# 1/rms spread one k step earlier, u_s copied out of PSUM by ScalarE, the first weight split moved ahead

## The chip, the cores and the metric

The kernel runs on one core of a Trainium2 chip. The metric is the device time of one execution in microseconds (us). Five engines work side by side, each through its own instructions in program order: PE (TensorE matmul, with PEld for its weight loads), DVE (VectorE), ACT (ScalarE), POOL (GpSimd) and SP (SyncE), whose queue issues every DMA of this kernel. An instruction that waits holds up everything behind it on its engine.

## The reference, cut to what matters

```python
h = rms_norm(x, pre_g)                       # x: 1024 x 1024, f32
proj = h @ w_in                              # cb | ca -> conv branch, u_s -> S5 branch, z and g gates
cu = ca * sigmoid(cb); cu = causal_depthwise_conv(cu)          # 31 taps
conv_out = (silu(layer_norm(cu)) * silu(z_c)) @ w_conv_out
y = gelu(s5(u_s)); y = y * sigmoid(y @ w_glu + b_glu)          # complex-diagonal state scan
ssm_out = (y * silu(z_s)) @ w_ssm_out
merged = sigmoid(g_c) * conv_out + sigmoid(g_s) * ssm_out
out = x + rms_norm(merged @ w_out, post_g)
```

## The kernel before, in words

Every f32 product is made of three passes of rounded operands: high part times high part, high times low, low times high. So each operand is split: ACT copies the high part (`xh`, `wh_...`), and DVE subtracts it from the original to get the low part (`xl`, `wl_...`). A product of one 128-channel block is 48 matmuls of 128x512: for each of 8 k steps a pair with (wh, xh), a pair with (wh, xl), a pair with (wl, xh).

The order is written out by hand in Python. A small clock object (`clk`) follows TensorE's time while the list `seq` of products is walked, and background chains (the S5 branch, the convolution taps, the LayerNorm) are put between the products' instructions when the clock says that their DVE cost and their delay have passed. A chain yields (cost, delay) pairs for that. Changing a delay therefore moves instructions in the program, not at run time.

The start has to overlap the norm with the first product. The three first u_s blocks (`usp0` to `usp2`, in PSUM) are multiplied from unnormalised x (raw x times the gain), 8 k steps of 9 passes. Meanwhile ACT squares x (`x_square`, on the second copy `xin`), DVE and POOL make 1/rms (`x_rms`, tile `r8t`), and in the eighth k step TensorE spreads it over the partitions (`x_spread`: matmuls into `rb`, then ACT copies `rb` to the tile `rbc`). Then

- `x_scale(k)` (DVE, L170) multiplies raw x by gain and `rbc`; `x_norm(k)` splits it anew (ACT `xh` L175, DVE `xl` L176), once the fourth u_s block `usp3` has used the raw `xh`, `xl` of that k;
- `us_out(m)` (DVE, L183) multiplies `usp{m}` by `rbc` out of PSUM into `usT{m}`, writes it to DRAM (`us_scratch`) and reads it back in 8 small DMAs as `U{m}` for S5;
- `wsplit_h`, `wsplit_l` (ACT L696, DVE L704) split the next weights of `order`: us3, cb0, ca0, gc0, cb1, ... ; `wload`, called at the end of `wsplit_l`, issues the load (`wr_...`) of the one two further on. There are two buffers for raw weights.

Products then follow as cb0, ca0, gc0, cb1, ca1, gc1, ... In `ln_stat(c)` the finished convolution block `acc{c}` is transposed by TensorE (`lnp{c}`) and DVE takes its statistics (`BN_STATS`). In `ln_chain` 1/std and mean are spread by TensorE (`lnr`, `lnm`), and DVE and ACT apply them to the eight blocks.

Of the kernel before, what the change touches and what calls it, by code (L numbers as in the profile page):

```python
# [10 lines left out]
AF = mybir.ActivationFunctionType  # L11
ALU = mybir.AluOpType
# [23 lines left out]
def tile_hybrid_block(  # L36
# [25 lines left out]
    V, A, G, PE = nc.vector, nc.scalar, nc.gpsimd, nc.tensor  # L62
# [14 lines left out]
    def T(name, dt=F32):  # L77
        return tp.tile([128, 1024], dt, tag="T", name=name)

    def PS(name, tag):  # L80
        return ps.tile([128, 1024], F32, tag=tag, name=name)

    def f32(t):
        return t.bitcast(F32)
# [27 lines left out]
    def load_xt(k):  # L112
        xraw[k] = T(f"xt{k}")
        nc.sync.dma_start(out=xraw[k], in_=xt[k])
# [4 lines left out]
    def us_weights(k2, parts=1):  # L119
        wusr[k2] = wp.tile([128, 1024], F32, tag="wraw", name=f"wusr{k2}", bufs=WRAW)  # L120
        n = 768 // parts
        for i in range(parts):
            nc.sync.dma_start(out=wusr[k2][:, i * n:(i + 1) * n], in_=w_us[k2][:, i * n:(i + 1) * n])
# [25 lines left out]
    def load_x(t):  # L149
        xin[t] = T(f"xin{t}")  # L150
        nc.sync.dma_start(out=xin[t], in_=xv[t])

    def x_square(t):
        xi = xin.pop(t)
        A.activation(out=xi, in_=xi, func=AF.Square, accum_out=ssq8[:, t:t + 1])
# [5 lines left out]
    def x_spread(rb):  # L161
        for t in range(8):
            PE.matmul(rb[:, t * 128:(t + 1) * 128], lhsT=r8t[:, t:t + 1].to_broadcast([128, 128]), rhs=ident,
                      start=True, stop=True)
        rbc = T("rbc")
        A.activation(out=rbc, in_=rb, func=AF.Copy)
        return rbc
# [10 lines left out]

    usU = {}

    def us_out(m, p, rbc):
        u = T(f"usT{m}")
        V.tensor_tensor(out=u, in0=p, in1=rbc, op=ALU.mult)  # L183
        clk.fg(1.2)
        nc.sync.dma_start(out=us_scr[m], in_=u)
        usU[m] = T(f"U{m}")
        src = us_scr[m].rearrange("(g h) (t n) -> t h g n", g=8, t=8)
        for t in range(8):
            nc.sync.dma_start(out=usU[m][16 * (7 - t):16 * (8 - t)].rearrange("p (g n) -> p g n", g=8), in_=src[t])
# [374 lines left out]
    stat_left, ln_done = [8], [False]  # L564

    def ln_stat(c):
        p = PS(f"lnp{c}", "aux")
        for t in range(8):
            PE.transpose(p[:, t * 128:(t + 1) * 128], acc[c][:, t * 128:(t + 1) * 128], ident)
        clk.now += 0.9  # L570
        yield 0.0, 2.0
        for t in range(8):
            V.bn_stats(out=st8[:, t, c, :], in_=p[:, t * 128:(t + 1) * 128])
            if t % 4 == 3:
                yield 0.9, 0.0
        stat_left[0] -= 1
        yield 0.0, 0.0
# [102 lines left out]
    def wload():  # L680
        if rnext[0] < len(order):
            u = order[rnext[0]]
            rnext[0] += 1
            src, kt = wsrc(*u)
            raw = wp.tile([128, 1024], F32, tag="wraw", name=f"wr_{u[0]}{u[1]}", bufs=WRAW)
            nc.sync.dma_start(out=raw[:, 0:kt * 128], in_=src)
            raws[u] = (raw, kt)

    def wsplit_h():
        if wnext[0] < len(order):  # L690
            u = order[wnext[0]]
            wnext[0] += 1
            raw, kt = raws.pop(u)
            n = kt * 128
            h = wp.tile([128, 1024], F32R, tag="wh", name=f"wh_{u[0]}{u[1]}", bufs=WHL)
            A.activation(out=h[:, 0:n], in_=raw[:, 0:n], func=AF.Copy)  # L696
            half[0] = (u, raw, h, n)

    def wsplit_l():
        if half[0]:  # L700
            u, raw, h, n = half[0]
            half[0] = None
            l = wp.tile([128, 1024], F32R, tag="wl", name=f"wl_{u[0]}{u[1]}", bufs=WHL)
            V.tensor_tensor(out=l[:, 0:n], in0=raw[:, 0:n], in1=f32(h[:, 0:n]), op=ALU.subtract)  # L704
            clk.fg(1.14 * n / 1024)
            wt[u] = (h, l)
            wload()
# [66 lines left out]
    def s5_chain():  # L774
        yield from s5_params(P5)
        for c in range(4):
            while not P5_ready[0]:
                yield 0.0, 0.5
            yield from s5_quarter(c, P5)
        for c in range(4):  # L780
            yh[c], yl[c] = T(f"yh{c}", F32R), T(f"yl{c}", F32R)
            A.activation(out=yh[c], in_=y32[c], func=AF.Copy)
            V.tensor_tensor(out=yl[c], in0=y32[c], in1=f32(yh[c]), op=ALU.subtract)
            yield 1.15, 0
        s5_done[0] = True
        yield 0.0, 0.0
# [5 lines left out]
    usp = {m: PS(f"usp{m}", "aux" if m == 2 else "mm") for m in range(3)}  # L792
# [3 lines left out]
    rbc = None  # L796
    for k in range(8):
        if k == 0:
            us_weights(2)
            load_xt(6)  # L800
            load_xt(7)
            for t in range(3):
                load_x(t)
            clk.add('s5', s5_chain())
        if k == 1:
            us_weights(3)
            for t in range(3, 8):
                load_x(t)
        if k == 2:
            for d_, s_ in ((chn, chan), (cw, conv_w), (iota, iota_in), (bgl, bglu), (bmt, bmat), (cmt, cmat),  # L810
                           (dmt, dmat)):
                nc.sync.dma_start(out=d_, in_=s_)
        if k + 2 < 8:
            x_raw(k + 2)
            if k % 2 == 0:
                us_split(k // 2 + 1, 0, 1)
        for t in {3: (0, 1), 4: (2, 3, 4), 5: (5, 6, 7)}.get(k, ()):
            x_square(t)
        if k == 5:
            x_rms()  # L820
        if k == 6:
            V.tensor_scalar(out=nb1, in0=chn[:, 0, :], scalar1=-1.0, scalar2=None, op0=ALU.mult)
            V.tensor_scalar(out=b2, in0=chn[:, 0, :], scalar1=2.0, scalar2=None, op0=ALU.mult)
            cwv = cw.rearrange("p c (r e) -> p c r e", e=2)
            V.tensor_tensor(out=hs, in0=cwv[:, :, :, 0], in1=cwv[:, :, :, 1], op=ALU.add)
            clk.fg(0.6)
        if k == 5:
            for _ in range(WRAW):
                wload()
        h, l = wus[k // 2]  # L830
        c0 = (k % 2) * 384
        kk = [slice(c0 + m * 128, c0 + m * 128 + 128) for m in range(3)]
        passes = ((h, xh), (l, xh), (h, xl))
        for n_, (m, i) in enumerate([(m, i) for i in range(3) for m in range(3)]):
            lhs, rhs = passes[i]
            for j in range(2):
                js_ = slice(j * 512, (j + 1) * 512)
                PE.matmul(usp[m][:, js_], lhsT=lhs[:, kk[m]], rhs=rhs[:, k, js_], start=(k == 0 and i == 0),  # L838
                          stop=(k == 7 and i == 2))
            if k == 7 and n_ == 0:  # L840
                rbc = x_spread(PS("rb", "aux"))
                wsplit_h()
                wsplit_l()
                clk.dve = max(clk.dve, clk.now + 1.5)
                for k_ in range(4):
                    x_scale(k_, rbc)
            clk.tick(0.45)
    us_out(0, usp[0], rbc)
    h, l = wt.pop(("us", 3))
    usp[3] = PS("usp3", "aux")  # L850
    for k in range(8):
        ks = slice(k * 128, (k + 1) * 128)
        for lhs, rhs, st, sp_ in ((h, xh, k == 0, False), (h, xl, False, False), (l, xh, False, k == 7)):
            for j in range(2):
                PE.matmul(usp[3][:, js(j)], lhsT=lhs[:, ks], rhs=rhs[:, k, js(j)], start=st, stop=sp_)
        x_norm(k)
        if k < 4:
            x_scale(k + 4, rbc)
        if k == 1:
            us_out(1, usp[1], rbc)  # L860
        if k == 3:
            wsplit_h()
            wsplit_l()
        clk.tick(1.296)
    us_out(2, usp[2], rbc)
    us_out(3, usp[3], rbc)
    P5_ready[0] = True
    clk.add('conv', conv_chain())

# [16 lines left out]
    for u in seq:  # L886
        kind, m = u
        report(u)
        if kind == "cb":
            p = proj(u)  # L890
# [5 lines left out]
        elif kind == "ca":  # L896
            p = proj(u)
# [6 lines left out]
        elif kind in ("gc", "zc"):  # L904
            p = proj(u)
# [8 lines left out]
        elif kind == "glu":  # L914
            p = product(f"pgl{m}", u, lambda k, j: yh[k][:, js(j)], lambda k, j: yl[k][:, js(j)])
# [5 lines left out]
        elif kind == "zs":  # L921
            p = proj(u)
# [11 lines left out]
        elif kind == "gs":  # L934
            p = proj(u)
# [4 lines left out]
        elif kind == "so":  # L940
            p = product(f"pso{m}", u, lambda k, j: y2h[k][:, js(j)], lambda k, j: y2l[k][:, js(j)])
# [26 lines left out]
        elif kind == "co":  # L968
# [5 lines left out]
            p = product(f"pco{m}", u, lambda k, j: cuh[:, k, js(j)], lambda k, j: cul[:, k, js(j)])  # L974
# [70 lines left out]
    for t in range(4, 7):  # L1045
        p = PS(f"po{t}", "aux" if t < 6 else "mm")
# [85 lines left out]
```

## Time and profile before

| | |
|---|---|
| median of 3 runs | 849.43 us (847.44 to 849.70) |
| the profiled execution | 848.62 us, of it 846.5 us span |
| PE busy | 820.1 us, 97% |
| DVE busy | 622.6 us, 74% |
| ACT busy | 276.1 us, 33% |
| DMA queue of SP | 90.17 MB |

The span is what the profile covers; the 2.1 us beside it lie before and after. PE busy is a modelled figure. A row of a timeline gives start, duration, engine, line, operation, out<-in, form and count, and in brackets the idle time of the engine just before it and what ended it. A row of the chain gives start, duration and what stood on the chain of waits that ended last.

### The profile page before, as it was taken

The numbers are of one execution on the slowest core, as the hardware profiler recorded it, in microseconds if no ns is written. First come the engines' busy times: TensorE is split into PE (matmuls) and PEld (weight loads), VectorE is DVE, ScalarE is ACT, GpSimd is POOL, SyncE is SP. The second block draws the span as 40 slices with busy tenths as digits, with TensorE's granted clock in tenths as the row PEclk, the third lists the DMA queues.
The fourth block names the chain that finished last, engine by engine and source line by source line (L and its number), as shares of the span: only waits on it lengthen the run. The fifth ranks groups of instructions, "written<-read, shape, count | busy, mean of one in ns | idle before, by whom it ended". The sixth has DMA issues, their size and how long they took to land.

```text
span 846.5 us, 9751 instructions
## 1 busy us (share of the span) xinstructions
PE 820.1 (97%) x3856; PEld 680.4 (80%) x3856; DVE 622.6 (74%) x902; ACT 276.1 (33%) x297; POOL 26.1 (3%) x26
## 2 busy tenths in 40 slices
PE   6979999999999999999989999999999999999996
PEld 5868888888788888888778888888878788888885
DVE  4597889889799899998879859589593644452242
ACT  5641344443524354314221221033262411122121
POOL 3400000000000000000000000000000000000010
PEclk9999999999999999999999999999999999999999
DMA  9635232341413302210112112212353343325142
GB/s 345 244 119 180 75 89 75 89 148 53 111 52 100 102 38 79 71 50 26 50 38 87 63 38 99 75 63 101 109 208 117 136 187 141 138 76 193 50 174 99
DMA packets 35180, 90.77 MB, mean 107 GB/s; under 512 B 8304, under 2 KB 13040, under 8 KB 35136
## 3 DMA queue, kind: packets, MB, share of 16 engines
q1 hardware_dynamic: 35136, 90.17, 31.5%
q8 instruction: 30, 0.49, 0.3%
q14 instruction: 14, 0.11, 0.0%
HBM read 65.90 MB, written 18.87 MB: 100 GB/s over the span
## 4 chain that ended last, share of the span: by engine, by line
PE 80%; DVE 13%; ACT 3%; issue 2%; DMA 1%; SPq 0%; DVEq 0%; POOLq 0%; ACTq 0%
PE pco L729 10%; PE po L1005 10%; PE pzc L729 9%; PE pgc L729 9%; PE pgs L729 9%; PE pca L729 8%; PE pcb L729 8%; PE pso L729 4%; PE usp L838 4%; PE pgl L729 3%; DVE pp L531 2%; DVE acc L531 1%; PE pzs L729 1%; DVE xt L170 1%; PE yp L484 1%
## 5 line engine op out<-in xcount | busy, mean ns | idle before, releaser
L531 DVE SCALAR_TENSOR_TENSOR pp<-ext,cw,pp 128x512 f32<-128x512 f32 x232 | 165.3, 748 | 10.4 <-ACT pp L522 10.4
L531 DVE SCALAR_TENSOR_TENSOR acc<-ext,hs,acc 128x512 f32<-128x512 f32 x120 | 89.8, 748 | 0.0
L1005 PE MATMUL po<-wox,mgh 128*128 128x512 f32 x192 | 52.3, 390 | 0.0
L729 PE MATMUL pcb<-xh,wl_cb 128*128 128x512 f32 x128 | 40.6, 399 | 6.1 <-DVE wl_cb L704 6.1
L507 ACT ACTIVATE ext<-ext 128x1179 f32<-128x1179 f32 x8 | 9.5, 1191 | 106.9 <-DVE ext L506 106.9
L1005 PEld LDWEIGHTS po<-wox,mgh 128*128 128x128 f32 x192 | 36.1, 188 | 7.5
L729 PE MATMUL pco<-cuh,wl_co 128*128 128x512 f32 x128 | 39.5, 390 | 1.3 <-DVE wl_co L704 1.3
L729 PE MATMUL pgs<-xh,wh_gs 128*128 128x512 f32 x128 | 39.6, 390 | 1.2 <-ACT gst L939 1.2
L729 PE MATMUL pcb<-xh,wh_cb 128*128 128x512 f32 x128 | 40.7, 400 | 0.0
L729 PE MATMUL pgc<-xh,wh_gc 128*128 128x512 f32 x128 | 40.5, 398 | 0.0
L729 PE MATMUL pca<-xh,wh_ca 128*128 128x512 f32 x128 | 39.9, 393 | 0.7 <-ACT wh_ca L696 0.7
L729 PE MATMUL pcb<-xl,wh_cb 128*128 128x512 f32 x128 | 40.2, 396 | 0.0
L729 PE MATMUL pzc<-xh,wh_zc 128*128 128x512 f32 x128 | 40.2, 396 | 0.0
L729 PE MATMUL pzc<-xh,wl_zc 128*128 128x512 f32 x128 | 39.6, 391 | 0.6 <-DVE Sx L476 0.6
L729 PE MATMUL pca<-xh,wl_ca 128*128 128x512 f32 x128 | 39.7, 392 | 0.1
L729 PE MATMUL pzc<-xl,wh_zc 128*128 128x512 f32 x128 | 39.5, 390 | 0.0
L729 PE MATMUL pgc<-xh,wl_gc 128*128 128x512 f32 x128 | 39.5, 390 | 0.0
L729 PE MATMUL pgc<-xl,wh_gc 128*128 128x512 f32 x128 | 39.5, 390 | 0.0
L729 PE MATMUL pca<-xl,wh_ca 128*128 128x512 f32 x128 | 39.5, 390 | 0.0
L729 PE MATMUL pco<-cul,wh_co 128*128 128x512 f32 x128 | 39.5, 390 | 0.0
L729 PE MATMUL pco<-cuh,wh_co 128*128 128x512 f32 x128 | 39.5, 390 | 0.0
L729 PE MATMUL pgs<-xh,wl_gs 128*128 128x512 f32 x128 | 39.5, 390 | 0.0
(266 smaller groups left out, 1740.2 us busy)
## 6 DMA issues: line engine op xcount, KB each, us to landing
xt<-in_xt_dram SPq DMA_DIRECT2D x8, 512.0 KB, 6.2
xin<-in_x_dram SPq DMA_DIRECT2D x8, 512.0 KB, 9.8
wr_cb<-in_w_in_dram SPq DMA_DIRECT2D x8, 512.0 KB, 3.3
wr_ca<-in_w_in_dram SPq DMA_DIRECT2D x8, 512.0 KB, 3.3
wr_gc<-in_w_in_dram SPq DMA_DIRECT2D x8, 512.0 KB, 3.3
gc_scratch<-gct SPq DMA_DIRECT2D x8, 512.0 KB, 2.6
wr_zc<-in_w_in_dram SPq DMA_DIRECT2D x8, 512.0 KB, 3.3
zc_scratch<-zct SPq DMA_DIRECT2D x8, 512.0 KB, 2.8
```

The source lines that it names most:

```text
L170: V.scalar_tensor_tensor(out=xraw[k], in0=xraw[k], scalar=gcol[:, k:k + 1], in1=rbc, op0=ALU.mult, op1=ALU.mult)
L484: PE.matmul(yp[:, s], lhsT=Sx[:, s], rhs=O1[:, s], start=False, stop=True)
L507: A.activation(out=ext[:, :, 0:3, 1:132], in_=ext[:, :, 4:7, 0:131], func=AF.Copy)
L531: V.scalar_tensor_tensor(out=o, in0=src(e, r), scalar=w, in1=o, op0=ALU.mult, op1=ALU.add)
L729: PE.matmul(p[:, js(j)], lhsT=lhs[:, ks], rhs=rhs(k, j), start=st, stop=sp_)
L838: PE.matmul(usp[m][:, js_], lhsT=lhs[:, kk[m]], rhs=rhs[:, k, js_], start=(k == 0 and i == 0), stop=(k == 7 and i == 2))
L1005: PE.matmul(p[:, js(j)], lhsT=lhs[k][:, s], rhs=rhs[k][:, js(j)], start=st, stop=sp_)
```

## The change

Five edits.

1. The squares of x are taken one k step earlier (k = 2 to 5 instead of 3 to 5), the last two ahead of the raw split of x's eighth block.
2. The split of us3's weights is moved into the seventh k step after the second pass, and `x_spread` with the first four `x_scale` into the seventh k step after the sixth pass; before, they stood in the eighth after the first.
3. `us_out` is divided: ACT copies `usp{m}` to SBUF (`us_copy`, three of them right after the k loop, the fourth after `usp3`), and DVE multiplies in SBUF, for all four blocks after the last split of x.
4. cb0's weights are split in the k steps 1 (high) and 2 (low) of `usp3` instead of both in step 3.
5. `ln_stat` begins with a delay of 3.5 us in the clock.

```diff
-    def us_out(m, p, rbc):
-        u = T(f"usT{m}")
-        V.tensor_tensor(out=u, in0=p, in1=rbc, op=ALU.mult)
+    def us_copy(m, p):
+        usT[m] = T(f"usT{m}")
+        A.activation(out=usT[m], in_=p, func=AF.Copy)
+
+    def us_out(m, rbc):
+        u = usT.pop(m)
+        V.tensor_tensor(out=u, in0=u, in1=rbc, op=ALU.mult)
...
     def ln_stat(c):
+        yield 0.0, 3.5
...
+        if k == 5:
+            x_square(6)
+            x_square(7)
         if k + 2 < 8:
             x_raw(k + 2)
...
-        for t in {3: (0, 1), 4: (2, 3, 4), 5: (5, 6, 7)}.get(k, ()):
+        for t in {2: (0,), 3: (1, 2, 3), 4: (4, 5)}.get(k, ()):
             x_square(t)
...
-            if k == 7 and n_ == 0:
-                rbc = x_spread(PS("rb", "aux"))
+            if k == 6 and n_ == 1:
                 wsplit_h()
                 wsplit_l()
+            if k == 6 and n_ == 5:
+                rbc = x_spread(PS("rb", "aux"))
...
-    us_out(0, usp[0], rbc)
+    for m in range(3):
+        us_copy(m, usp[m])
...
         if k == 1:
-            us_out(1, usp[1], rbc)
-        if k == 3:
             wsplit_h()
+        if k == 2:
             wsplit_l()
         clk.tick(1.296)
-    us_out(2, usp[2], rbc)
-    us_out(3, usp[3], rbc)
+    us_copy(3, usp[3])
+    for m in range(4):
+        us_out(m, rbc)
```

On DVE, from the fourth `x_scale` to the low half of cb0's weights, before:

```order
L170 SCALAR_TENSOR_TENSOR xt3_112<-xt3_112,gcol_89,rbc_437 128x1024
L183 TENSOR_TENSOR usT0_465<-usp0_124,rbc_437 128x1024
L176 TENSOR_TENSOR xl_94<-xt0_100,xh_93 128x1024
L170 SCALAR_TENSOR_TENSOR xt4_117<-xt4_117,gcol_89,rbc_437 128x1024
L176 TENSOR_TENSOR xl_94<-xt1_106,xh_93 128x1024
L170 SCALAR_TENSOR_TENSOR xt5_119<-xt5_119,gcol_89,rbc_437 128x1024
L183 TENSOR_TENSOR usT1_496<-usp1_125,rbc_437 128x1024
L176 TENSOR_TENSOR xl_94<-xt2_108,xh_93 128x1024
L170 SCALAR_TENSOR_TENSOR xt6_139<-xt6_139,gcol_89,rbc_437 128x1024
L176 TENSOR_TENSOR xl_94<-xt3_112,xh_93 128x1024
L170 SCALAR_TENSOR_TENSOR xt7_141<-xt7_141,gcol_89,rbc_437 128x1024
L704 TENSOR_TENSOR wl_cb0_528<-wr_cb0_331,wh_cb0_526 128x1024
```

And the same stretch of DVE after:

```order
L170 SCALAR_TENSOR_TENSOR xt3_112<-xt3_112,gcol_89,rbc_423 128x1024
L176 TENSOR_TENSOR xl_94<-xt0_100,xh_93 128x1024
L170 SCALAR_TENSOR_TENSOR xt4_117<-xt4_117,gcol_89,rbc_423 128x1024
L176 TENSOR_TENSOR xl_94<-xt1_106,xh_93 128x1024
L170 SCALAR_TENSOR_TENSOR xt5_119<-xt5_119,gcol_89,rbc_423 128x1024
L176 TENSOR_TENSOR xl_94<-xt2_108,xh_93 128x1024
L170 SCALAR_TENSOR_TENSOR xt6_139<-xt6_139,gcol_89,rbc_423 128x1024
L711 TENSOR_TENSOR wl_cb0_489<-wr_cb0_331,wh_cb0_478 128x1024
```

The two `usT` products left the stretch, and `wl_cb0` now stands before the fourth `xl` and the eighth `x_scale`.

On SP's queue, from the load of ca0's raw weights to that of ca1's, before:

```order
L686 DMA wr_ca0_443<-in_w_in_dram 128x1024
L185 DMA us_scratch<-usT0_465 128x1024
L189 DMA U0_468<-us_scratch 16x8x128 x8
L185 DMA us_scratch<-usT1_496 128x1024
L189 DMA U1_499<-us_scratch 16x8x128 x8
L686 DMA wr_gc0_530<-in_w_in_dram 128x1024
L185 DMA us_scratch<-usT2_564 128x1024
L189 DMA U2_567<-us_scratch 16x8x128 x8
L185 DMA us_scratch<-usT3_576 128x1024
L189 DMA U3_579<-us_scratch 16x8x128 x8
L686 DMA wr_cb1_623<-in_w_in_dram 128x1024
L686 DMA wr_ca1_712<-in_w_in_dram 128x1024
```

And after, from the load of gc0's raw weights:

```order
L693 DMA wr_gc0_491<-in_w_in_dram 128x1024
L191 DMA us_scratch<-usT0_453 128x1024
L195 DMA U0_538<-us_scratch 16x8x128 x8
L191 DMA us_scratch<-usT1_455 128x1024
L195 DMA U1_549<-us_scratch 16x8x128 x8
L191 DMA us_scratch<-usT2_457 128x1024
L195 DMA U2_560<-us_scratch 16x8x128 x8
L191 DMA us_scratch<-usT3_534 128x1024
L195 DMA U3_571<-us_scratch 16x8x128 x8
L693 DMA wr_cb1_615<-in_w_in_dram 128x1024
L693 DMA wr_ca1_716<-in_w_in_dram 128x1024
```

gc0's load moved ahead of the u_s round trips; cb1's load stays behind all four of them, which now begin with the `usT0` product at the end of the x splits.

On PE, the transposes of the fifth convolution block, before (in the middle of `pca5`):

```order
L729 MATMUL pca5_3209<-xl_94,wh_ca5_3165 128x512 x2
L729 MATMUL pca5_3209<-xh_93,wl_ca5_3181 128x512 x2
L569 MATMUL lnp4_3257<-ident_78,acc4_2944 128x128 x8
L729 MATMUL pca5_3209<-xh_93,wh_ca5_3165 128x512 x2
L729 MATMUL pca5_3209<-xl_94,wh_ca5_3165 128x512 x2
```

And after (behind the last matmuls of `pca5`, ahead of the next product):

```order
L736 MATMUL pca5_3205<-xl_94,wh_ca5_3161 128x512 x2
L736 MATMUL pca5_3205<-xh_93,wl_ca5_3177 128x512 x2
L576 MATMUL lnp4_3279<-ident_78,acc4_2940 128x128 x8
L736 MATMUL pgs0_3288<-xh_93,wh_gs0_3230 128x512 x2
L736 MATMUL pgs0_3288<-xl_94,wh_gs0_3230 128x512 x2
```

`lnp4` moved back by three k steps, 18 matmuls.

More of the change, by code (lines that the diff above doesn't have):

```diff
@@ L179, in tile_hybrid_block @@
     usU = {}
-    def us_out(m, p, rbc):
-        u = T(f"usT{m}")
-        V.tensor_tensor(out=u, in0=p, in1=rbc, op=ALU.mult)
+    usT = {}
+    def us_copy(m, p):
[4 more added lines that the diff above has]
+        V.tensor_tensor(out=u, in0=u, in1=rbc, op=ALU.mult)
         clk.fg(1.2)
```

## The prediction

> **What bounds the kernel.** I read the page's engine line first, then the chain of waits, then the timelines of PE, DVE and SP around the places where PE is idle. The page says that PE is nearly always busy:
>
> ```profile
> PE 820.1 (97%) x3856; PEld 680.4 (80%) x3856; DVE 622.6 (74%) x902; ACT 276.1 (33%) x297; POOL 26.1 (3%) x26
> ```
>
> So only the few idle stretches of PE can be won. The longest after the start lies in the first product on normalised x. The chain of waits (start, duration, what) runs through DVE there:
>
> ```profile
> 38.73 1.80 PE rb L163 x16
> 40.55 1.03 ACT rbc L166
> 42.56 1.23 DVE wl_us L704
> 43.78 4.78 DVE xt L170 x4
> 48.56 1.14 DVE usT L183
> 49.70 1.08 DVE xl L176
> ...
> 60.15 1.14 DVE wl_cb L704
> 61.34 12.64 PE pcb L729 x44
> ```
>
> PE's timeline at that place, and the granted clock (eighth value, PEclk) in three windows:
>
> ```profile
> 54.90 0.61 PE L729 MATMUL pcb<-xh,wh_cb 128*128 128x512 f32 x2
> 55.35 0.62 PE L729 MATMUL pcb<-xl,wh_cb 128*128 128x512 f32 x2
> 61.34 1.22 PE L729 MATMUL pcb<-xh,wl_cb 128*128 128x512 f32 x2 [5.38 <-DVE wl_cb L704]
> ...
> 66.55 0.62 PE L729 MATMUL pcb<-xh,wl_cb 128*128 128x512 f32 x2
> ...
> 73.82 0.62 PE L729 MATMUL pca<-xh,wh_ca 128*128 128x512 f32 x2
> ...
> 59.60:59.70 0.10, 0.00 (x0) 0.00 (x0) 0.10 (x1) 0.00 (x0) 0.00 (x0) 0.57 0.00 0
> 66.40:66.60 0.20, 0.20 (x2) 0.16 (x2) 0.20 (x1) 0.00 (x0) 0.00 (x0) 0.90 0.75 307
> 432.00:434.00 2.00, 1.23 (x9) 1.04 (x10) 2.00 (x5) 0.00 (x0) 0.00 (x0) 1.00 0.00 0
> ```
>
> PE stands for 5.38 us until the low half of cb0's weights is there. From 66.55 to 73.82 it issues 16 pairs, 0.4535 us each, so a product of 24 pairs takes 10.88. From 61.34 to 66.55 the six pairs take 5.21 instead of 2.72: the clock fell to half at 59.6, 3.65 after PE stopped, and came back at 66.4. Wait and slow restart cost 5.38 + 2.49 = 7.9 us; without them pca would start at 54.90 + 10.88 = 65.78, 8.0 before 73.82.
>
> **The spread (edits 1 and 2).** These rows say when 1/rms is ready and where the seventh k step's last three passes begin:
>
> ```profile
> 34.48 1.64 POOL L159 TENSOR_TENSOR r8t<-ssq,mhalf 128x8 f32<-128x8 f32 x1 [5.08 <-DVE spt L243]
> 36.76 1.52 PE L838 MATMUL usp<-xl,wush 128*128 128x512 f32 x6
> 45.58 1.06 ACT L175 ACTIVATE xh<-xt 128x1024 fp32r<-128x1024 f32 x1 [3.05 <-PE usp L855]
> ```
>
> r8t was ready at 36.12. The squares stand earlier on ACT but x's last raw split later, and r8t waits behind that on DVE; I put it between 35.4 and 36.3, before 36.76, so the spread does not hold PE. It runs at 36.76 instead of 38.57, rbc ends at 39.8, and with us3's split already done DVE can begin x_scale near 40.1 instead of 43.7 and end the four at 44.9. What is late next is ACT: its three u_s copies, some 0.93 each, start when usp0 is complete (43.3) and push xh0 from 45.58 to 46.1. It ends at 47.15, DVE idles 2.3 us for it, and xl0 starts at 47.15 instead of 49.70.
>
> **The low half of cb0 (edits 3 and 4).** From there DVE does three xl (1.14) and three x_scale (1.20, a quarter of 4.78): wl_cb0 starts at 54.15 and ends at 55.37. PE wants it for the third pair, 54.90 + 0.91 = 55.81. So the 8.0 us are won here, with 0.4 us to spare. The rest of the splits keep ahead: the last xl ends at 62.2, wanted at 64.9.
>
> **What comes late next: ca0.** Behind wl_cb0 stand five xl, one x_scale and now all four usT products (4 x 1.14) ahead of wl_ca0. usT0 starts at 54.15 + 1.14 + 5.70 + 1.20 = 62.2, wl_ca0 at 66.75, and it ends at 67.95. pca's third pair wants it at 66.69: a new wait of 1.3 us. pca ends at 65.78 + 1.3 + 10.88 = 77.96; gc0, with eight transposes (half of rb's 1.80) in it, ends at 89.7.
>
> **And then cb1.** Its raw weights are loaded behind the u_s round trips in SP's queue. SP before, and the landing time of cb1's load:
>
> ```profile
> 49.73 0.33 SPq L185 DMA_DIRECT2D us_scratch<-usT  x1
> ...
> 56.12 0.38 SPq L185 DMA_DIRECT2D us_scratch<-usT  x1
> ...
> 64.40 0.38 SPq L686 DMA_DIRECT2D wr_gc<-in_w_in_dram  x1
> 66.99 0.34 SPq L185 DMA_DIRECT2D us_scratch<-usT  x1
> ...
> 73.36 0.36 SPq L185 DMA_DIRECT2D us_scratch<-usT  x1
> ...
> 80.12 0.37 SPq L686 DMA_DIRECT2D wr_cb<-in_w_in_dram  x1
> ...
> DMA to landing us min/median/max: 3.2/3.2/3.2
> ```
>
> One round trip takes 6.39, 8.28, 6.37 and 6.76 us (differences of the starts). The new first one starts when usT0 ends, 62.2 + 1.22 = 63.4, 13.7 later than before, and all four follow without a gap: 3 x 6.38 + 6.76 = 25.9. cb1's load is issued at 89.3 and lands at 92.5; gc0's no longer waits in that queue. The split and PE's use of it before:
>
> ```profile
> 88.00 1.05 ACT L696 ACTIVATE wh_cb<-wr_cb 128x1024 fp32r<-128x1024 f32 x1
> 89.18 1.22 DVE L704 TENSOR_TENSOR wl_cb<-wr_cb,wh_cb 128x1024 fp32r<-128x1024 f32 x1
> 96.48 0.62 PE L729 MATMUL pcb<-xh,wh_cb 128*128 128x512 f32 x2
> 97.39 0.62 PE L729 MATMUL pcb<-xh,wl_cb 128*128 128x512 f32 x2
> ```
>
> Now wh_cb1 ends at 93.6: PE, ready at 89.7, waits 3.8 us, and the third pair waits for wl_cb1 until 94.9. Before it ran at 97.39. Of the 8.0 won, 1.3 go at ca0 and some 4.2 at cb1; 2.5 stay, if the clock holds. A slow restart has the bounds 0 (the window at 432, where a wait of 1.95 kept 1.00) and the 2.49 above. The wait of 3.8 is nearer to 5.38 and just beyond 3.65, but the clock came back 5.1 after the restart, so its steps follow no fixed delay, and 3.8 barely reaches; I take 0 and keep the other as a rival.
>
> The Trainium skill (TensorE: Matmul & The Clock Gate, Part 1: The HAM clock gate) has the clock fall after one whole idle window of about 3.4 us that runs free of the kernel. By that, an estimate, a wait of 3.8 holds a whole window in about (3.8 - 3.4) / 3.4 = 0.12 of the cases, and the sum would mostly be the one taken here. The trace agrees in that fall and return lie 6.8 us apart, two such windows; no run here shows a wait of 3.8.
>
> What waits behind wl_cb1 on DVE (taps and S5's first quarter) starts 4.5 us later than before. Its cover is DVE's later idle time; one such row carries the rest:
>
> ```profile
> 158.71 1.23 DVE L435 TENSOR_TENSOR tk<-ta,tb 128x1024 f32<-128x1024 f32 x1
> 162.64 0.28 DVE L440 TENSOR_TENSOR kr<-kp,dmt 16x128 f32<-16x128 f32 x1 [2.71 <-ACT kr L439]
> ```
>
> By then DVE is back in step and waits 2.71 for PE's kp, so S5 can follow a PE that is 2.5 ahead, just. Were it not, PE would give the difference back later.
>
> **ln_stat's delay (edit 5).** In PE's order it moves four sets of lnp transposes (lnp4 to lnp7) back by three k steps (18 matmuls, 4.1 us), lnp0's forward, and on DVE the statistics behind them. Rows of PE's later waits and what stands before them:
>
> ```profile
> 377.08 4.85 DVE L573 BATCH_NORM_STATS2 st<-lnp 128x6 f32<-128x128 f32 x24 [1.35 <-PE lnp L569]
> 413.11 0.73 PE L729 MATMUL pcb<-xh,wl_cb 128*128 128x512 f32 x2 [0.70 <-DVE wl_cb L704]
> 432.50 0.33 PE L569 MATMUL lnp<-ident,acc 128*128 128x128 f32 x1 [1.95 <-DVE acc L539]
> 626.03 1.25 ACT L615 ACTIVATE acc<-acc,chn 128x1024 f32<-128x1024 f32 x1 [2.48 <-DVE acc L614]
> 629.53 1.02 ACT L939 ACTIVATE gst<-pgs 128x1024 f32<-128x1024 f32 x1
> 630.61 0.73 PE L729 MATMUL pgs<-xh,wh_gs 128*128 128x512 f32 x2 [1.15 <-ACT gst L939]
> ```
>
> Of the 24 statistics at 377.08, lnp3's eight go behind acc4's end (a third of 4.85, 1.6 us): DVE reaches wl_cb5 and acc4 1.6 earlier, and the 0.70 goes. lnp4 at 432.50 comes 4.1 later in PE's order than an acc4 that was 1.95 late: that wait goes whole. At 630.61 PE waits for gst5 to leave PSUM, on ACT behind the Silu of acc5; in the new order gst5 stands ahead of it. The LN spread comes 2.7 later, but two splits of weights pass it, and I find gst5 done 1.0 before PE wants it: 1.15 won. Bounds for the three together: 0 and 3.8; I take 3.8, for each has its margin (0.8, 2.2, 1.0).
>
> **The sum.** 2.5 + 3.8 = 6.3 us off the profiled execution's 848.62 gives 842.3. That execution lay 0.81 below the median of the runs, 849.43; against the median it is 843.1.
>
> **The rivals.**
> - The clock falls at cb1's wait. For it: 3.8 is beyond the 3.65 after which it fell. The seventh pair would run at 93.6 + 5.21 = 98.8 instead of 96.48 + 2.72 = 99.2: 0.4 stays of 2.5, and the time is 845.2.
> - The late waits only move: BN_STATS and LN are as long as before, so PE meets them elsewhere, or DVE's S5 chain cannot use the 2.5. Against it: DVE idles 2.71 and 1.35 in the rows above. One of the two terms remains, 845.6 to 846.9; both lost is 849.4.
> - Slower: SP's round trips take 8.28 each, like the second one. cb1's load is issued at 63.4 + 33.1 = 96.5, wh_cb1 ends at 100.8, after 11 us of waiting with a slow restart; the seventh pair runs at 106.0 instead of 99.2, 6.8 lost less 3.8, 852.4. It decides from 7.5 us a trip. Against it: the other three took 6.4 to 6.8, and now no weight load runs between them.
> - That the spread is no earlier, because r8t is late: each us up to 2.3 is covered by the wait for xh0, so it changes little.
>
> **Chances.** Forecast 0.46; clock falls 0.22; late waits move 0.18, mostly within the bound; slower 0.08; better, near 840, if other short waits go too, 0.06. A measurement of this kernel tells about 0.3%, 2.5 us, from no change: below 846.9 is faster, above 852.0 slower. Faster 0.46 + 0.22 + 0.06 + 0.04 of the third = 0.78, same 0.14, slower 0.08. The range takes in the clock and one lost term: 840.8 to 847.4.
>
> **What would show it.** Right: no PE wait at pcb0 near 55.8 and clock 1.00 there; a wait of about 1.3 at pca0 for wl_ca; a wait of 3 to 5 at pcb1 for wh_cb, with cb1's load issued near 89; no wait at lnp4. Wrong: cb1's load issued well before 85 or after 94, a clock of 0.50 behind it, or waits of PE beyond 1 us between 100 and 430.

## The result and the profile after

| | before | changed |
|---|---|---|
| median | 848.95 us (847.44 to 849.70) | 843.77 us (843.01 to 844.81) |
| ratio | | 0.9942, 95% interval 0.9923 to 0.9961 |
| the profiled execution | 848.62 us, span 846.5 | 844.35 us, span 842.6 |

The change made the kernel faster by 0.58%; forecast were 843.1 us and a range of 840.8 to 847.4. The total fits, but by luck: of the terms behind it, the start lost where a gain was forecast, and the late waits gave more. The page's engine line of the changed kernel, and its table of who waited for whom (engine, line, what it waited for, us in total, times, longest):

```profile
PE 819.7 (97%) x3856; PEld 681.1 (81%) x3856; DVE 622.1 (74%) x902; ACT 279.6 (33%) x301; POOL 25.8 (3%) x26
...
PE usp L848 <- ACT wush L132: 7.2, 1, 7.2
PE pcb L736 <- ACT wh_cb L703: 5.6, 1, 5.6
PE pco L736 <- DVE wl_co L711: 1.3, 1, 1.3
PE pca L736 <- DVE wl_ca L711: 1.1, 1, 1.1
PE pzc L736 <- DVE Sx L482: 0.5, 1, 0.5
PE po L1017 <- DVE wl_wo L711: 0.2, 1, 0.2
```

The wait for cb0's low half is gone, and those at lnp4 and pgs with it; one for the high half of cb1 has come. PE's timeline at the start of the program, and the granted clock (PEclk, eighth value) around the new wait:

```profile
55.29 0.62 PE L736 MATMUL pcb<-xh,wh_cb 128*128 128x512 f32 x2
...
56.20 0.62 PE L736 MATMUL pcb<-xh,wl_cb 128*128 128x512 f32 x2
...
66.17 0.62 PE L736 MATMUL pca<-xh,wh_ca 128*128 128x512 f32 x2
68.36 0.72 PE L736 MATMUL pca<-xh,wl_ca 128*128 128x512 f32 x2 [1.12 <-DVE wl_ca L711]
...
89.81 0.63 PE L736 MATMUL pgc<-xh,wl_gc 128*128 128x512 f32 x2
96.02 1.22 PE L736 MATMUL pcb<-xh,wh_cb 128*128 128x512 f32 x2 [5.58 <-ACT wh_cb L703]
...
94.70:94.80 0.10, 0.00 (x0) 0.00 (x0) 0.00 (x0) 0.00 (x0) 0.00 (x0) 0.67 1.16 451
101.40:101.50 0.10, 0.10 (x2) 0.10 (x1) 0.10 (x2) 0.00 (x0) 0.00 (x0) 0.50 0.81 328
```

pcb0's third pair runs at 56.20 without a wait: the edits do there what they say. At pcb1 PE stands for 5.58 us; the clock falls to half at 94.7, 4.3 after PE's last matmul had ended, and comes back just after 101.5. SP's queue and ACT say why the wait is long:

```profile
63.79 0.33 SPq L191 DMA_DIRECT2D us_scratch<-usT  x1
70.20 0.37 SPq L191 DMA_DIRECT2D us_scratch<-usT  x1
77.07 0.37 SPq L191 DMA_DIRECT2D us_scratch<-usT  x1
84.14 0.34 SPq L191 DMA_DIRECT2D us_scratch<-usT  x1
87.77 3.62 SPq L195 DMA_DIRECT2D U<-us_scratch  x8
91.48 0.37 SPq L693 DMA_DIRECT2D wr_cb<-in_w_in_dram  x1
...
94.91 1.06 ACT L703 ACTIVATE wh_cb<-wr_cb 128x1024 fp32r<-128x1024 f32 x1 [10.81 <-DMA wr_cb<-in_w_in_dram]
```

The four round trips take 6.41, 6.87, 7.07 and 7.34 us, 27.7 together instead of the 25.9 of the forecast, and began 0.4 later. When PE begins each product, in both profiled executions (from the timelines, us from the span's start):

| first pair of | before | changed | difference |
|---|---|---|---|
| pcb0 | 54.90 | 55.29 | +0.39 |
| pca0 | 73.82 | 66.17 | -7.65 |
| pgc0 | 84.70 | 78.48 | -6.22 |
| pcb1 | 96.48 | 96.02 | -0.46 |
| pca1 | 111.43 | 113.65 | +2.22 |
| pca2 | 229.09 | 230.69 | +1.60 |
| pcb5 | 411.34 | 412.84 | +1.50 |
| pca5 | 423.21 | 423.72 | +0.51 |
| pgs0 | 438.03 | 435.40 | -2.63 |
| pgs6 | 630.61 | 626.77 | -3.84 |
| first po | 752.05 | 748.08 | -3.97 |

At the end of the start PE is 2.2 us **behind** the kernel before. From there to the end it wins 6.2: 0.6 at pca2, 1.0 at pcb5, 3.1 at lnp4, 1.4 at pgs.

### The profile page after: what moved, and what is told of

Read it like the earlier page. It is cut to its first block, busy times and chain, and to the rows that moved or that the text cites. A ratio compares the mean times of both kernels' runs of the same rounds, so it can differ in the third digit from the quotient of the medians.

```text
span 842.6 us, 9753 instructions
## 1 busy us (share of the span) xinstructions
PE 819.7 (97%) x3856; PEld 681.1 (81%) x3856; DVE 622.1 (74%) x902; ACT 279.6 (33%) x301; POOL 25.8 (3%) x26
## 4 chain that ended last, share of the span: by engine, by line
PE 81%; DVE 10%; ACT 3%; DMA 2%; issue 2%; SPq 1%; DVEq 0%; POOLq 0%; ACTq 0%
PE pgs L736 10%; PE pzc L736 10%; PE pco L736 10%; PE po L1017 10%; PE pcb L736 8%; PE pca L736 8%; PE pzs L736 5%; PE pso L736 5%; PE usp L848 4%; PE pgc L736 4%; PE pgl L736 3%; DVE pp L537 1%; DVE xl L176 1%; DMA Zw<-Zs 1%; PE lnp L576 1%
## 5 line engine op out<-in xcount | busy, mean ns | idle before, releaser
L1033 DVE TENSOR_TENSOR o<-po,postg 128x1024 f32<-128x1024 f32 (+1 forms) x9 | 10.0, 1106 | 40.3 <-ACT q L1032 40.3
```

Of the source, the lines that this page charges most:

```text
L1033: V.tensor_tensor(out=o[:, s], in0=p, in1=pog[:, s], op=ALU.mult)
```

## The experiments

Medians, and ratios to the kernel before, run beside each:

| kernel | us | ratio, 95% interval |
|---|---|---|
| edit 5 alone | 844.85 | 0.9958 (0.9946 to 0.9971) |
| edits 1 to 4 | 851.34 | 1.0033 (1.0020 to 1.0046) |
| changed, cb1's load first | 836.13 | 0.9857 (0.9842 to 0.9872) |
| the same, ca0's split first too | 834.96 | 0.9844 (0.9830 to 0.9857) |
| cb1's load first, without edit 5 | 841.03 | 0.9914 (0.9900 to 0.9928) |
| changed, half of the last reads behind cb1's load | 843.89 | 0.9938 (0.9925 to 0.9950) |
| cb1's load first, spread late | 839.53 | 0.9891 (0.9877 to 0.9904) |
| ca0 and cb1 first, spread two passes later, co0's split first | 835.37 | 0.9843 (0.9829 to 0.9856) |
| spread late, planner's clock 0.5 back | 838.42 | 0.9878 (0.9864 to 0.9891) |
| ca0 and cb1 first, co0's split first | 832.94 | 0.9815 (0.9802 to 0.9828) |
| edit 5 alone, planner's clock 0.5 back | 843.79 | 0.9943 (0.9929 to 0.9956) |

### Edit 5 alone, and edits 1 to 4 alone

```diff
     def ln_stat(c):
+        yield 0.0, 3.5      # on the kernel before; taken out again from the changed one
         p = PS(f"lnp{c}", "aux")
```

> The kernel before with edit 5 alone. By the prediction's terms it wins 3.8 us: 845.1 against 848.95. By the trace after, where the three late waits cost PE 5.6 with the slow pair behind each (0.99 + 3.14 + 1.45), it wins 5.6: 843.4, as fast as the whole change, and the waits at lnp4 and pgs are gone from the profile. If the late waits had gone only because the changed kernel's PE came 1.5 us later to them, edit 5 alone wins under 1: 848 to 849.

> Edits 1 to 4 without edit 5. By the prediction's terms it wins 2.5 us: 846.5. By the trace after, PE is 2.2 us behind the kernel before when pca1 starts if the clock falls at pcb1's wait, and level with it if not, and of the later waits only those of 0.6 and 0.7 at pca2 and pcb5 can go: 848.5 to 850.5, no faster than before, with the wait at lnp4 near 2 us still in the profile.

Edit 5 alone wins 3.4 us, near the 3.8 of the prediction. Edits 1 to 4 lose 3.1, where the prediction had a gain of 2.5: its term for the start had the wrong sign. PE's waits in the profile of edits 1 to 4:

```profile
97.12 1.22 PE L735 MATMUL pcb<-xh,wh_cb 128*128 128x512 f32 x2 [7.10 <-ACT wh_cb L702]
...
415.58 0.72 PE L735 MATMUL pcb<-xh,wl_cb 128*128 128x512 f32 x2 [0.69 <-DVE wl_cb L710]
434.98 0.33 PE L575 MATMUL lnp<-ident,acc 128*128 128x128 f32 x1 [1.96 <-DVE acc L545]
...
634.52 0.73 PE L735 MATMUL pgs<-xh,wh_gs 128*128 128x512 f32 x2 [0.96 <-ACT gst L950]
```

The wait at pcb1 is 7.10 here and was 5.58 in the changed kernel, with the same instructions ahead of it in SP's queue. Executions vary that much: the four round trips took 28.5 instead of 27.7, the load landed after 4.0 instead of 3.3, and PE came 0.4 earlier. The two parts together make -3.4 + 3.1 = -0.3, the whole change -5.2; the last experiments go into what is missing.

Edit 5 alone did not take the late waits as the prediction had it either. Its profile keeps the one at pca2 (0.66) and has a new one of 0.73 at pca5, right behind pcb5, where the old 0.70 has gone:

```profile
229.73 0.74 PE L730 MATMUL pca<-xh,wh_ca 128*128 128x512 f32 x2 [0.66 <-ACT wh_ca L697]
...
424.98 0.74 PE L730 MATMUL pca<-xh,wl_ca 128*128 128x512 f32 x2 [0.73 <-DVE wl_ca L705]
```

### cb1's load ahead of three round trips, and ca0's split ahead of three products

`us_out` is divided into its product and `us_trip` (the write and the eight reads); `wsplit_l` calls what `late` holds.

```diff
-    for m in range(4):
-        us_out(m, rbc)
+    for m in range(4):           # first kernel: only SP's order changes
+        us_out(m, rbc)
+    us_trip(0)
+    late.append(lambda: [us_trip(m) for m in (1, 2, 3)])
...
+    us_out(0, rbc)               # second kernel: the products too
+    us_trip(0)
+    for m_ in (1, 2, 3):
+        late.append(lambda m=m_: (us_out(m, rbc), us_trip(m)))
...
             wload()
+            if late:
+                late.pop(0)()
```

> The changed kernel, only the order of SP's queue changed: cb1's load behind the first u_s round trip instead of behind all four. The load is issued near 70.5 instead of 91.5, so wh_cb1 is there before PE is (90.3), the wait of 5.6 us at pcb1 and the half clock behind it go. If the load behind the round trips is the whole cause: 5.6 + 0.3 + about half of 2.3 (the clock fell in some runs only) = 7 off, 836.8, provided DVE's S5 and convolution work follows a PE that is 7 earlier. If DVE sets the middle of the program, PE meets its waits there again (at pcb5, lnp, Sx) and 841 to 843.8 remains. If not the load but the split on ACT or DVE was late, the wait stays near 5.

> As the run before, and the u_s products 1 to 3 with their round trips stand one by one behind the low halves of ca0, gc0 and cb1 on DVE: wl_ca0 ends near 65, before pca's third pair wants it at 67.1, and the wait of 1.1 goes too. Without a bound in the middle 1.4 less than the run before (835.4); with DVE as the bound there the same as the run before within 1 us.

836.13 and 834.96, within 0.7 of what was expected for the load as the whole cause. SP, ACT and PE of the first:

```profile
70.26 0.38 SPq L696 DMA_DIRECT2D wr_cb<-in_w_in_dram  x1
...
84.08 1.04 ACT L706 ACTIVATE wh_cb<-wr_cb 128x1024 fp32r<-128x1024 f32 x1
...
89.84 0.62 PE L741 MATMUL pgc<-xh,wl_gc 128*128 128x512 f32 x2
90.31 0.62 PE L741 MATMUL pcb<-xh,wh_cb 128*128 128x512 f32 x2
```

The load is issued 21 us earlier, ACT splits it at its place in the program and PE goes from pgc0 to pcb1 without a gap. PE is then 6.2 us ahead of the kernel before at pca1 (105.25 against 111.43) and 12.4 at the first po (739.61 against 752.05): DVE follows, so that the middle of the program sets no bound at this size. The stall at pcb1 had eaten the whole gain of edits 1 to 4 and more. The expectation took it that the clock had fallen in some runs of the changed kernel only. Their mean granted clocks are 0.993 to 0.995 in all four runs, 0.998 to 0.999 in the four of this kernel, and 0.997 at the lowest in any profile without a fall; so it fell in all four.

### How long must PE wait before the clock falls?

Four of the eight reads of the last u_s block are put behind cb1's load.

```diff
+        read(range(4 if m == 3 else 8))
+        if m == 3:
+            late.append(lambda: read(range(4, 8)))
```

> The changed kernel with four of the eight reads of the last u_s block put behind cb1's load, which is issued 4 x 0.45 = 1.8 us earlier: PE's wait at pcb1 is near 3.8, as the prediction had it, instead of 5.6. By the prediction's step the clock holds at 1.00 there, and the first pairs after the wait stand 0.45 us apart: 841.3. If the clock still falls, they stand 0.85 apart for up to 6.8 us and the time is 842.7 (1.8 off and no more).

843.89, no different from the changed kernel: neither number came out, because the wait did not become 3.8. SP, ACT, PE and the clock:

```profile
89.61 0.37 SPq L697 DMA_DIRECT2D wr_cb<-in_w_in_dram  x1
90.03 1.85 SPq L196 DMA_DIRECT2D U<-us_scratch  x4
...
94.20 1.06 ACT L707 ACTIVATE wh_cb<-wr_cb 128x1024 fp32r<-128x1024 f32 x1 [10.09 <-DMA wr_cb<-in_w_in_dram]
...
95.31 1.22 PE L742 MATMUL pcb<-xh,wh_cb 128*128 128x512 f32 x2 [4.91 <-ACT wh_cb L707]
...
94.70:94.80 0.10, 0.00 (x0) 0.00 (x0) 0.00 (x0) 0.10 (x1) 0.00 (x0) 0.74 1.14 292
98.10:98.20 0.10, 0.10 (x2) 0.10 (x1) 0.10 (x1) 0.10 (x1) 0.00 (x0) 0.69 0.30 123
```

The load went out 1.9 us earlier, but from issue to split it took 4.6 us instead of 3.4, and the wait shrank by only 0.67. That the four reads issued right behind it slowed it is likely but not shown: in the profile of edits 1 to 4 the same load, with no read behind it, took 4.1. The clock fell again, 4.3 us after PE's last matmul, this time for 3.4 us and not 6.8. A wait of 3.8 was not reached. But other profiles show that such a wait is not safe: with edits 1 to 4 the clock fell at 92.1, only 2.1 us after PE's last matmul ahead of pcb1, and behind lnp4 it fell after waits of 2.2 in all (next section, and the last one).

### Is it the spread, or the planner?

First the kernel with cb1's load first, without edit 5; then with edit 5 but with edits 1 and 2 undone; then that one and the kernel before with edit 5, each with only the planner's DVE clock set back at the end of the start:

```diff
+    clk.dve -= 0.5
     P5_ready[0] = True
     clk.add('conv', conv_chain())
```

> The kernel with cb1's load first (836.13) without edit 5. Edit 5 was worth 3.4 us on the kernel before and 7.6 on edits 1 to 4. If its own worth is the 3.4 and the rest came from the stall at pcb1 and the clock in those executions, this kernel gives 836.1 + 3.5 = 839.6, with waits at pcb5 (0.7), lnp4 (2.0) and pgs (1.0). If edits 1 to 4 make the late waits longer by themselves (the DVE order that the planner writes), it gives 843.5 or more.

> The kernel with cb1's load first (836.13), with edits 1 and 2 undone: the spread stands in the eighth k step again, x_scale starts near 43.7 instead of 40.2. By the prediction's step xl0 then starts at 48.5 instead of 47.5, since it had waited 2.5 for xh0 before; wl_cb0 ends at 56.7 against 56.2 wanted, a wait under 1 us, and 0.55 of wait for r8t goes: 836.2 to 837. If the 3.5 us of the spread count whole, wl_cb0 ends 3.5 later, a wait of 2.7 at pcb0: 839 to 840.

> The kernel with the late spread (839.53) with one number changed: the planner's DVE clock is set back by 0.5 us at the end of the start, so that the planner puts the transposes lnp0 at the end of zc1, as in the changed kernel, and not into the first glu product. The start on the chip stays as it was, 1.5 us behind the kernel with cb1's load first (836.13). If the other 2 us between those two kernels come from the planner's order, this gives 837.6 and the waits at pca2 (0.67) and pca5 (0.73) go; if they come from the start being later, it stays at 839.5.

> The kernel before with edit 5 (844.85) and the planner's DVE clock set back by 0.5 us at the end of the start: on the chip the start is that of the kernel before. If the order that the planner writes was what edits 1 and 2 changed for the late waits, the waits at pca2 and pca5 go and it gives 842.9, faster than the whole change (843.77); if not, 844.9.

Without edit 5 it is 841.03, 4.9 slower: between its 3.4 on the kernel before and its 7.6 on edits 1 to 4. The profile of this kernel shows the waits expected, and a fall of the clock that was not (windows of time, PE's busy time first, PEclk eighth):

```profile
425.76 0.33 PE L578 MATMUL lnp<-ident,acc 128*128 128x128 f32 x1 [1.96 <-DVE acc L548]
426.36 1.75 PE L578 MATMUL lnp<-ident,acc 128*128 128x128 f32 x7 [0.27 <-DVE acc L550]
...
422.75:426.10 3.35, 1.38 (x6) 0.69 (x4) 3.35 (x8) 0.00 (x0) 0.00 (x0) 1.00 0.00 0
426.20:429.50 3.30, 3.14 (x11) 2.85 (x12) 2.59 (x9) 0.00 (x0) 0.00 (x0) 0.50 0.24 84
```

The profile of edits 1 to 4 has the same behind its lnp4 (half clock from 436.9 to 440.3): pca5 and lnp4 take 16.42 there (425.70 to 442.12) against 14.82 in the kernel before. That 1.6 and the 1.5 us more of wait at pcb1 are, in these profiles, most of the 4.2 by which edit 5 seemed worth more on edits 1 to 4 than on the kernel before; the new wait at pca5, which edit 5 alone has and the changed kernel has not, makes up about the rest. Of the four runs without edit 5 the profiled one took 843.15, the others 840.96 to 841.09; the mean granted clock is 0.997 in all four, which does not tell whether it fell in the others too.

With the spread late, 839.53, as the rival expected; but not for its reason. The profile has the wait of the prediction's step:

```profile
57.35 0.73 PE L741 MATMUL pcb<-xh,wl_cb 128*128 128x512 f32 x2 [0.79 <-DVE wl_cb L714]
69.90 0.73 PE L741 MATMUL pca<-xh,wl_ca 128*128 128x512 f32 x2 [1.37 <-DVE wl_ca L714]
...
224.41 0.73 PE L741 MATMUL pca<-xh,wh_ca 128*128 128x512 f32 x2 [0.67 <-ACT wh_ca L706]
...
372.46 4.85 DVE L583 BATCH_NORM_STATS2 st<-lnp 128x6 f32<-128x128 f32 x24 [1.39 <-PE lnp L579]
```

At pgc0 PE is 1.5 us behind the kernel with the early spread (80.01 against 78.52). From pcb0 to pgc0 it takes 24.5 against 23.2, so 1.3 is what the 3.5 us earlier spread is worth there. Ahead of pcb0 two other things nearly cancel: the slow start of the program (last section) lasted 1.0 longer in this execution, and the kernel with the early spread waits 0.6 for r8t. The other 2.2 are lost between 220 and 440, at pca2 and pca5, as with edit 5 alone. Both have 24 statistics in one piece on DVE, the changed kernel 16, because the planner put lnp0 elsewhere. In PE's program order, without edit 5 (early spread), and with edit 5 (late spread):

```
565 L740 MATMUL pzc1_2002<-xh_93,wl_zc1_1961 128x512 x2
566 L578 MATMUL lnp0_2014<-ident_78,acc0_797 128x128 x8

729 L741 MATMUL pgl0_2481<-yh3_2405,wl_glu0_2452 128x512 x2
730 L579 MATMUL lnp0_2526<-ident_78,acc0_797 128x128 x8
731 L741 MATMUL pgl1_2536<-yh0_2381,wh_glu1_2488 128x512 x2
```

So edits 1 and 2 moved lnp0, through the planner's clock; not edit 5. Setting that clock back by 0.5 alone puts lnp0 into pzc1 as well (in the trace behind its first k step, not at its end, as the expectation has it). It won 1.1 us on each of the two kernels (838.42 and 843.79): half of the 2 expected, since the waits at pca2 and pca5 (0.67 and 0.73) are gone and others of 0.54, 0.20 and 0.37 have come. The kernel before with two numbers of its planner changed is as fast as the whole change (0.9943 against 0.9942).

### A better kernel

On the kernel with ca0 and cb1 first: co0's low half is split ahead of the first convolution splits on DVE, with the spread two passes later, and without that.

```diff
                 wsplit_h()
+                if u == ("so", 7):
+                    wsplit_l()
...
-            if k == 6 and n_ == 5:    # in the first kernel only
+            if k == 6 and n_ == 7:
```

> The kernel with ca0 and cb1 first (834.96), the low half of co0's weights put ahead of the first convolution splits on DVE, and the spread two passes later in the seventh k step: the waits of 1.33 at pco and 0.3 at rb go with 0.3 of slow pairs behind the first: 833.0. If cul0 then comes late at pco's second pair, the wait only changes its name, and 834.7 remains.

> The kernel with ca0 and cb1 first (834.96), with the low half of co0's weights ahead of the first convolution splits on DVE and nothing else; all ahead of the last so product keeps its order. The wait of 1.33 at pco goes with 0.3 of slow pairs: 833.4. If cul0 comes late instead: 834.9.

835.37 and 832.94. In the first, the later spread won nothing at the start but the wait for r8t, 0.3 in the kernel with ca0 and cb1 first: from the sixth group of matmuls to pgc0 PE takes 60.30, the same as in the second, which leaves the spread where it was and has no wait for r8t in its profile. But moving the spread moved the planner's clock, and the wait at pgs was back:

```profile
619.38 0.73 PE L741 MATMUL pgs<-xh,wh_gs 128*128 128x512 f32 x2 [1.16 <-ACT gst L960]
```

The second left the plan alone and is the fastest: 1.85% below the kernel before. Its table of waits:

```profile
PE usp L853 <- ACT wush L132: 7.4, 1, 7.4
PE pzc L741 <- DVE Sx L485: 0.6, 1, 0.6
PE po L1026 <- DVE wl_wo L714: 0.2, 1, 0.2
```

## Why the prediction was right, and where its steps were not

The forecast was 6.3 us off the profiled execution: 2.5 at the start, 3.8 late. Measured in the profiles: -2.2 and 6.2, together 4.0 of the span (of the medians, 5.2). Two errors of opposite sign, 4.7 and 2.4, so that the total came out near the forecast is luck.

- **The spread and the low half of cb0**: right, step by step. DVE began x_scale at 40.19 (40.1), xl0 waited for xh0 behind the u_s copies and started at 47.54 (47.15), and from pcb0 to pca0 PE took 8.0 less, as predicted. The rival that the spread is covered by the wait for xh0 is mostly right too: 3.5 us of it are worth 1.3.
- **ca0**: 1.12 of wait and 1.43 of time, against 1.3.
- **cb1**: the place and the cause are right, and the kernel with its load moved shows it. The step that failed is the size: the round trips were taken at 6.38 and 6.76, from three of the four that the profile of before showed; they took 27.7. All four of before, with the slow one of 8.28, make 27.8. The wait was 5.58 instead of 3.8.
- **The clock**: "I take 0 and keep the other as a rival" is the step that failed most; a clock of 0.50 behind the load was also one of the prediction's own signs of being wrong. The clock fell in all three profiles with this wait (the changed kernel, edits 1 to 4, half of the reads moved), and from pcb1 to pca1 the changed kernel took 2.7 longer than the kernel before (17.63 against 14.95). The Trainium skill (TensorE: Matmul & The Clock Gate, Part 1: The HAM clock gate) has the clock halved for windows of about 3.4 us that run free of the kernel. The trace agrees with the length: half clock for 6.8 us in the changed kernel, 3.4 in the one with half of the reads moved. By its rule a wait of 5.58 holds a whole window in (5.58 - 3.4) / 3.4 = 0.64 of the cases, an estimate; it fell in all four runs. Their spans are 841.2, 841.4, 842.6 and 843.0, with mean granted clocks of 0.995, 0.993, 0.994 and 0.994, which do not part the two groups; what does is not known.
- **The late waits**: 3.8 was the sum of the idle times. At those three places 5.6 went (1.0, 3.1, 1.45), since a wait costs some 0.3 to 0.5 more than its bracket (below), and the prediction had left out 0.27 at lnp4. A further 0.6 went at pca2, which it did not name. What it says of edit 5 and lnp0 is wrong: edits 1 and 2 moved that. Its reason for the 0.70 at pcb5 did not hold either: with edit 5 alone DVE still takes 24 statistics in one piece, and the low half of ca5 starts at 423.71, against 423.09 before in an execution that ran 0.6 ahead. DVE had won no time there, and the wait came back at pca5.
- **The rivals**: that the clock falls at cb1's wait happened. Its 845.2, or 844.4 for the profiled execution, which took 844.35, is near by luck as well: it kept 0.4 of the start, where 2.2 were lost, and it had 3.8 for the late waits, which gave 6.2. That the late waits only move happened with edit 5 alone (pca5 for pcb5), with the late spread and with the spread shifted by two passes, and not in the changed kernel. The round trips came to 6.9 us on average, under the 7.5 from which the whole change would have been slower; without edit 5, and with the falls of the clock, edits 1 to 4 were slower (7.1 on average in that profile).

## What to carry to other kernels

When a change takes a stall away, look at what the same queue issues next, and sum all the durations that the profile shows, the slow one too: here the usual ones gave 25.9 and all four 27.8, for 27.7 measured. A load that does not depend on the round trips belongs ahead of them. A total that fits proves no term; run the halves of a change apart. Where a planner's clock places background work, an edit early in the program moves the waits of the far end by a microsecond or two, and a first trial that changes only the planner's number tells that from the edit itself.

## What the runs showed of the hardware that was not expected

- The clock fell behind waits of 1.96 + 0.27 us (edits 1 to 4 with cb1's load first): in the 3.35 us before the fall PE was busy for 1.38, 41%. The same waits in the kernel before kept 1.00. The Trainium skill (TensorE: Matmul & The Clock Gate, Part 1: The HAM clock gate) has the clock fall after at least one idle window; here a window in which PE was busy for part of the time was enough.
- The clock's steps lie on a grid, which fits with there being no fixed delay between wait and fall, as the prediction saw. In the profile of edits 1 to 4 the clock steps at 92.12, 102.36, 436.87 and 440.28, which lie 3, 98 and 1 times 3.413 us apart; in the kernel before it steps at 59.61 and 66.44, 2 times 3.413 apart. Counted on in such windows, the kernel before has a boundary at 431.67, in the middle of its wait at lnp4, and PE is busy for two thirds of the window on either side. Two windows of before, then the one ahead of the fall at pcb1 with edits 1 to 4 (PE's busy time first, PEclk eighth):

```profile
428.25:431.67 3.42, 2.30 (x11) 1.56 (x9) 3.42 (x7) 0.00 (x0) 0.00 (x0) 1.00 0.00 0
431.67:435.08 3.41, 2.31 (x13) 1.91 (x14) 3.41 (x10) 0.00 (x0) 0.00 (x0) 1.00 0.00 0
...
88.71:92.12 3.41, 1.31 (x6) 0.74 (x4) 0.00 (x0) 0.00 (x0) 0.00 (x0) 1.00 0.42 118
```

  Windows that were 38% and 47% busy (pcb1 and lnp4 with edits 1 to 4) and 40% (lnp4 with cb1's load first) were followed by a fall, two of 67% were not. So the same wait can cost nothing or a slow stretch, by where the boundary lies in it. That the share of busy time decides fits these windows; no run isolates it.
- A wait costs PE more than the idle time in its bracket. From the third pair of pcb5 to pca5 the profile of before has a wait of 0.70 and lost 1.0 against the changed kernel; at lnp4 2.22 of wait made 3.1. The bracket begins where the last matmul is modelled to end, some 0.17 after the next would have been issued (0.62 long, 0.4535 apart), and the first pair after a wait takes 0.56 to 0.58 instead of 0.4535.
- The first matmuls run at half pace (the first six take 2.73 us, later ones 1.36, from start to start), and how long that lasts differs between executions. The second group of six, in the kernel before and in the changed one (timeline, start and duration):

```profile
10.02 2.38 PE L838 MATMUL usp<-xh,wusl 128*128 128x512 f32 x6
...
9.91 2.77 PE L848 MATMUL usp<-xh,wusl 128*128 128x512 f32 x6
```

  The sixth group begins 9.07 us after the first one in the kernel before and 9.57 in the changed one, and between 8.30 and 9.70 in all profiles. From there to pcb0 both kernels take 38.54, so the 0.4 by which pcb0 came late in the changed kernel is this and not the change. PEclk reads 1.00 in this stretch, so that the clock makes the half pace is not shown.
